# Two-layer hybrid trunk: gate products of three branches as seven block products of summed operands, in place of eight

## The chip, the cores and the metric

One core of one Trainium2 chip. The metric is the device time of one execution in microseconds, as the median of three runs: 1218.11 us before the change (1217.89 to 1218.78). TensorE does the matrix products, ScalarE (ACT), VectorE (DVE) and GpSimd (POOL) the elementwise work, and SyncE (SP) starts most transfers.

## The reference, cut to what matters

```python
for l in range(2):                      # x: 512 latent positions, xc: 256 context positions, 1024 features
    h, hc = modulated_norm(x, xc)       # scale, shift and gate from c and c_ctx (called ada below)
    o_a, o_d, o_b, o_c = attention, windowed attention, Fourier mix, spatial gate   # 256 features each
    y = 0
    for r in (a, d, b, c):              # the merge
        y += sigmoid(h @ w_merge[r] + b_merge[r]) * ((o_r * silu(z_r)) @ w_br[r])
    x = x + gt * (y @ w_out)            # the context has the same, in layer 0 only
```

For each branch, `h @ w_merge[r]` is a product of 1024 features by 1024 outputs over all positions. These gate products are the largest part of the work.

## The kernel before

Features lie on the 128 partitions, positions along the free dimension: columns 0 to 255 are the context, 256 to 767 the latents. Layer 0 works on all 768 columns, layer 1 on the 512 latent ones. Every product is made of three matmuls on rounded parts: weights and activations are split into a high part in fp32r and a low part that is the rest, and `mm3` (L182) issues high x high, high x low and low x high.

Weights come as tiles of 128 x 512 (four blocks of 128 x 128) in the order of a list `plan` (L136). `wload` (L154) starts their transfers on SP's queue, `wround` (L162) splits them: ACT casts the high part (L169), and POOL, or DVE for every third tile, subtracts it (L171). `wnext` (L174) hands out the next tile, five loads and two splits ahead. There are three raw tiles, three high and three low ones.

`merge(r)` (L646) handles one branch in eight steps j, one for each 128 outputs. A step takes two weight tiles of 512 for the gate (8 x 3 matmuls over the latents into bank `gl`, and in layer 0 as many over the context into `gc`) and one of 256 for the branch (2 x 3 matmuls into `yl` and `gc`). Then ACT applies tanh (L669), DVE multiplies by the branch's product, which it reads from PSUM (L671), and the result is added to M: on POOL (L674), or on DVE in the last branch, where the sum is also split into MH and ML for the output product (L680, L681).

The order of the work is written as generators. `drive` (L865) alternates a main thread with a filler: each yield of the main thread adds to a balance, and the filler runs until its own yields, counted as 1.27 per column and triple of matmuls, have used it up. While the two attentions are the main thread (L936), a unit of one head and one query block pays PACE (L27: 4500 and 4000), and the filler is projections, branch C's merge, branch B's input and, last, branch A's merge (L929). What remains of the filler then runs alone (L945). Behind it, branches D and B are merged as the main thread (L951, L954), and the side work is paid 0.42 (SIDE, L31) of what a merge yields. In layer 0 the side is the Fourier mix `fnet` and then `ada_rest` (L248): its rows come as tiles of 128 x 512, and each yield of 1000 stands for one tile and two dot products on DVE (L274), one for each of two vectors. In layer 1 the side is `fnet` alone. The compiler's planner turns this into one order per engine, mostly by when operands are ready in its own estimate; the engines then run in that order.

## Time and profile before

| What | Value |
|---|---|
| Median of three runs | 1218.11 us (1217.89 to 1218.78) |
| The profiled execution, its own time | 1220.09 us |
| Span of the profiled execution, first to last instruction | 1218.2 us |
| TensorE busy | 1183.5 us (97%) |
| DVE busy | 658.7 us (54%) |
| ACT busy | 470.7 us (39%) |
| POOL busy | 392.2 us (32%) |
| Mean granted TensorE clock | 0.994 of full speed |
| Moved by DMA | 131.99 MB, mean 108 GB/s |

All durations below are from the profiled execution. A record's duration includes time that the instruction spends held up after it began. Matmuls overlap in their records, so the time of one is read from the distance of two starts. Times on POOL are rough in the profiler's own words, so they too are best read from start to start.

### The profile page before, as it was taken

What the parts mean: (1) busy time and instruction counts of PE and PEld (TensorE: products, weight loads), DVE (VectorE), ACT (ScalarE), POOL (GpSimd) and SP (SyncE); (2) the same over time, 40 slices, a digit from 0 to 9 for tenths busy, and PEclk for the clock granted to TensorE, in tenths of its full rate; (3) what the DMA queues carried; (4) which work ended last, traced back from release to release, by engine and by line L of the source; (5) the groups of instructions that cost most, each with busy time, mean ns of one, the idle gap of its engine ahead of it and who ended that gap; (6) DMA issues with size and microseconds to landing.
All of it is one profiled execution on the core that took longest, in us unless ns stands there. A gap on an engine that the chain in (4) does not pass through costs nothing.

```text
span 1218.2 us, 18950 instructions
## 1 busy us (share of the span) xinstructions
PE 1183.5 (97%) x7164; PEld 1004.2 (82%) x7164; DVE 658.7 (54%) x1325; ACT 470.7 (39%) x933; POOL 392.2 (32%) x292
## 2 busy tenths in 40 slices
PE   5999999999999999999999998989999999999998
PEld 3798888888888888888888887877788888888887
DVE  5673446443455442588988667646645554232331
ACT  5334634333333332322333255445444444333431
POOL 1322333212212234454222234442222233454332
PEclk8999999999999999999999999999999999999999
DMA  7717213211111113345555653373322212333353
GB/s 282 256 31 172 79 37 83 73 36 61 53 44 49 44 56 83 93 153 160 180 165 193 183 163 110 117 194 75 99 62 69 71 56 77 101 87 100 95 166 124
DMA packets 73499, 131.99 MB, mean 108 GB/s; under 512 B 8769, under 2 KB 19137, under 8 KB 73409
## 3 DMA queue, kind: packets, MB, share of 16 engines
q1 hardware_dynamic: 66640, 120.30, 33.8%
q10 hardware_dynamic: 6768, 10.50, 2.8%
q8 instruction: 56, 0.92, 0.3%
q14 instruction: 35, 0.28, 0.1%
HBM read 115.03 MB, written 4.19 MB: 98 GB/s over the span
## 4 chain that ended last, share of the span: by engine, by line
PE 86%; DVE 5%; DMA 4%; issue 2%; ACT 2%; POOL 1%; SPq 1%; ACTq 0%; POOLq 0%
PE gl L185 10%; PE gl L186 10%; PE gl L188 10%; PE o L631 4%; PE gc L185 3%; PE tp L598 3%; PE gc L188 3%; PE gc L186 3%; PE ow L185 3%; PE ow L186 3%; PE ow L188 3%; PE yl L185 2%; PE yl L186 2%; PE yl L188 2%; PE p L185 2%; PE p L188 2%
## 5 line engine op out<-in xcount | busy, mean ns | idle before, releaser
L171 POOL TENSOR_TENSOR wl<-wr,wh 128x512 fp32r<-128x512 f32 (+1 forms) x222 | 287.5, 1297 | 703.7 <-ACT wh L169 665.4
L169 ACT CAST wh<-wr 128x512 fp32r<-128x512 f32 (+1 forms) x320 | 184.5, 577 | 354.3 <-PE gl L186 92.4
L185 PE MATMUL gl<-hh,wh 128*128 128x512 f32 x512 | 204.2, 399 | 0.0
L186 PE MATMUL gl<-hl,wh 128*128 128x512 f32 x512 | 200.2, 391 | 0.0
L188 PE MATMUL gl<-hh,wl 128*128 128x512 f32 x512 | 199.9, 391 | 0.0
L574 DVE TENSOR_REDUCE mx<-s 128x1 f32<-128x768 f32 (+3 forms) x80 | 61.6, 770 | 131.5 <-PE s L568 67.4
L171 DVE TENSOR_TENSOR wl<-wr,wh 128x512 fp32r<-128x512 f32 (+1 forms) x98 | 68.9, 703 | 116.8 <-ACT wh L169 116.5
L188 PEld LDWEIGHTS gl<-hh,wl 128*128 128x128 f32 x512 | 96.1, 188 | 21.1
L185 PEld LDWEIGHTS gl<-hh,wh 128*128 128x128 f32 x512 | 96.5, 188 | 16.6 <-issue 0.2
L186 PEld LDWEIGHTS gl<-hl,wh 128*128 128x128 f32 x512 | 96.5, 189 | 16.2
L274 DVE CUSTOM_DVE_ANT_0 aj<-at,cb 128x512 f32<-128x512 f32 x128 | 107.1, 876 | 1.5 <-DMA at<-in_wadat_dram 1.5
L582 ACT ACTIVATE p<-s,ng 128x768 f32<-128x768 f32 (+3 forms) x80 | 60.1, 751 | 97.1 <-DVE ng L579 55.5
L185 PE MATMUL gc<-hh,wh 128*128 128x256 f32 x256 | 73.5, 287 | 0.0
L188 PE MATMUL gc<-hh,wl 128*128 128x256 f32 x256 | 72.5, 283 | 0.0
L186 PE MATMUL gc<-hl,wh 128*128 128x256 f32 x256 | 72.3, 283 | 0.0
L185 PE MATMUL p<-hh,wh 128*128 128x512 f32 (+1 forms) x192 | 71.1, 370 | 0.2 <-DVE z L539 0.2
L185 PE MATMUL ow<-MH,wh 128*128 128x512 f32 (+1 forms) x200 | 69.5, 348 | 1.3 <-DVE nq1a L343 0.9
L188 PE MATMUL ow<-MH,wl 128*128 128x512 f32 (+1 forms) x200 | 69.4, 347 | 0.9 <-DVE wl L171 0.9
L186 PE MATMUL ow<-ML,wh 128*128 128x512 f32 (+1 forms) x200 | 69.4, 347 | 0.0
L188 PE MATMUL p<-hh,wl 128*128 128x512 f32 (+1 forms) x192 | 68.4, 356 | 0.0
L186 PE MATMUL p<-hl,wh 128*128 128x512 f32 (+1 forms) x192 | 68.1, 355 | 0.0
L669 ACT ACTIVATE g<-gl,bmh 128x512 f32<-128x512 f32 x64 | 43.8, 685 | 62.2 <-DVE macc L274 37.0
(466 smaller groups left out, 2583.6 us busy)
## 6 DMA issues: line engine op xcount, KB each, us to landing
wr<-in_wm_dram SPq DMA_DIRECT2D x128, 256.0 KB, 2.7
wr<-in_win_dram SPq DMA_DIRECT2D x72, 256.0 KB, 2.9
at<-in_wadat_dram SPq DMA_DIRECT2D x64, 256.0 KB, 2.8
wr<-in_wo_dram SPq DMA_DIRECT2D x40, 256.0 KB, 3.0
aw<-in_wada_dram SPq DMA_DIRECT2D x16, 512.0 KB, 5.8
wr<-in_wm_dram SPq DMA_DIRECT2D x64, 128.0 KB, 2.2
ks<-yk SPq DMA_DIRECT2D x32, 192.0 KB, 4.2
wr<-in_wkv_dram SPq DMA_DIRECT2D x16, 256.0 KB, 2.7
```

Of the source, the lines that this page charges most:

```text
L169: A.copy(hi[:, :n], raw[:, :n])
L171: (V if on_v else G).tensor_sub(lo[:, :n], raw[:, :n], hi[:, :n].bitcast(F32))
L185: T.matmul(d, wh, xh[:, c0:c1], start=first and op, stop=False)
L186: T.matmul(d, wh, xl[:, c0:c1], start=False, stop=False)
L188: T.matmul(d, wl, xh[:, c0:c1], start=False, stop=last and cl)
L274: V.tensor_tensor_reduce(out=junk[:, :512], in0=w[:, :512], in1=cb[2 * v + half][:, :512], scale=0.5, scalar=0.0, op0=ALU.mult, op1=ALU.ad ...
L574: V.reduce_max(out=mx, in_=sv, axis=AX.X)
L582: A.activation(p[:, :nk], sv, AF.Exp, bias=ng, scale=0.125, accum_out=sm_)
L598: T.transpose(tp[:, (i - g0) * P:(i - g0 + 1) * P], p[:, i * P:(i + 1) * P], ident)
L631: T.matmul(dst[64 * hx:64 * hx + 64, :], vt[kt_ // 3][:, kt_ % 3, c0:c0 + 64], pts[hx][:, j * P:(j + 1) * P], start=(j == 0), stop=(j == l ...
L669: A.activation(g[:, q0:q1], gp, AF.Tanh, scale=0.5, bias=bmh[:, r * 8 + j:r * 8 + j + 1])
```

## The change

The gate products of branches A, D and B go from eight block products to seven, by the scheme of Strassen and Winograd. Outputs are taken in pairs (j, j+4), inputs in halves of four slices, and the columns are halved: 384 in layer 0, 256 in layer 1. For each pair, four tiles of weights are summed (two sums on DVE, two on POOL) to give seven tiles of 512 to split in place of four, and seven products of 4 x 3 matmuls over half the columns replace eight. ACT and DVE combine them in three PSUM banks and the gate tiles. The summed activations (`combos`) are made once per layer, with their own high and low parts. Branch C keeps the former merge.

Branch A leaves the attention's filler and is merged behind the attention with D and B, all three with the side work beside them. PACE goes down to 3250 in both layers. There are six raw weight tiles in place of three. `ada_rest` makes only one dot product per tile for the last eight rows of layer 1, whose second value nothing reads. To make room, the rotation's tables are loaded twice per layer into tiles of the z pool, and parts of M, ada's vectors and the next layer's input take tiles of other pools.

The core of the diff (the lists `loads` and `items` replace `plan`: an item is what is split, with its engine in `on_v`):

```diff
-PACE = (4500, 4000)
+PACE = (3250, 3250)
...
-LOADS, W_RAW, W_HI, W_LO = 5, 3, 3, 3
+LOADS, W_RAW, W_HI, W_LO = 5, 6, 3, 3
...
+        def merged_s(l, r):
+            def parts(j):
+                return [(wm[l, r, j, :, :512], 512), (wm[l, r, j, :, 512:1024], 512)]
+            def four(j):
+                (a, b), (c, d) = parts(j), parts(j + 4)
+                return [a, b, c, d]
+            ids = [[load(*x) for x in four(0)]]
+            ys = []
+            for j in range(4):
+                more = four(j + 1) if j < 3 else []
+                y0 = load(wm[l, r, j, :, 1024:], 256)
+                nxt = [load(*x) for x in more[:1]]
+                y1 = load(wm[l, r, j + 4, :, 1024:], 256)
+                nxt += [load(*x) for x in more[1:]]
+                ids.append(nxt)
+                ys.append((y0, y1))
+            for j in range(4):
+                a11, a12, a21, a22 = ids[j]
+                s1 = []
+                def prep(a11=a11, a12=a12, a21=a21, a22=a22, s1=s1):
+                    t = tl("p", f"s1_{a11}")[:, :512]
+                    V.tensor_add(t, raws[a21], raws[a22])
+                    G.tensor_sub(raws[a21], raws[a11], raws[a21])
+                    V.tensor_sub(raws[a11], t, raws[a11])
+                    G.tensor_sub(raws[a12], raws[a12], raws[a11])
+                    s1.append(t)
+                item(a11, 512, on_v=False)
+                item(a12, 512, on_v=True)
+                item(a22, 512, prep, lambda k=a11: raws[k], on_v=False)
+                item(a22, 512, None, lambda k=a21: raws[k], on_v=l == 1)
+                item(a22, 512, None, lambda s1=s1: s1[0], on_v=False)
+                item(ys[j][0], 256, on_v=False)
+                item(a22, 512, None, lambda k=a12: raws[k], on_v=True)
+                item(a22, 512, on_v=False)
+                item(ys[j][1], 256, on_v=False)
...
             for r in (R_A, R_D, R_B):
-                plan += merged(l, r)
-            plan += outw(l)
+                merged_s(l, r)
...
             i = cnt[0]
             cnt[0] += 1
-            wload(i + LOADS)
+            wload(max(k for k, *_ in items[i:i + LOADS]))
             wround(i + 2)
+            while prepped[0] < min(i + 3, len(items)):
+                prep = items[prepped[0]][2]
+                if prep:
+                    prep()
+                prepped[0] += 1
...
-                    for v in range(2):
+                    for v in range(1 if l and j >= 16 else 2):
...
+            HN = (WC.stop - WC.start) // 2
+            H1, H2 = slice(WC.start, WC.start + HN), slice(WC.start + HN, WC.stop)
+            BO = {}
+            def combos():
+                t23 = [[[tl("k", f"T{n}{part}{i}{l}", F32R) for i in range(2)] for part in "hl"] for n in (2, 3)]
+                t4 = [pq.tile([P, 2, NT], F32R, name=f"T4{part}{l}", tag="q") for part in "hl"]
+                def at(ts, kk):
+                    return [t[kk // 2][:, (kk % 2) * HN:(kk % 2) * HN + HN] for t in ts]
+                for n in (11, 21, 22, 1, 2, 3, 4):
+                    BO[n] = []
+                for kk in range(4):
+                    fa, fb = tl("sc", f"fa{l}{kk}"), tl("p", f"fb{l}{kk}")
+                    for f, k_ in ((fa, kk), (fb, kk + 4)):
+                        (V if f is fa else G).tensor_add(f[:, WC], hh[k_][:, WC].bitcast(F32), hl[k_][:, WC].bitcast(F32))
+                    V.tensor_sub(fa[:, H1], fa[:, H2], fa[:, H1])
+                    V.tensor_sub(fa[:, H2], fb[:, H2], fa[:, H2])
+                    V.tensor_sub(fb[:, H2], fb[:, H2], fa[:, H1])
+                    V.tensor_sub(fb[:, H1], fb[:, H1], fb[:, H2])
+                    one = [hh[kk][:, H2], hl[kk][:, H2]]
+                    two, three = at(t23[0], kk), at(t23[1], kk)
+                    four = [t[:, kk // 2, (kk % 2) * HN:(kk % 2) * HN + HN] for t in t4]
+                    for n, (hi, lo), src in ((2, two, fb[:, H2]), (3, three, fa[:, H2]), (1, one, fa[:, H1]),
+                                             (4, four, fb[:, H1])):
+                        A.copy(hi, src)
+                        (G if n < 3 else V).tensor_sub(lo, src, hi.bitcast(F32))
+                        BO[n].append((hi, lo))
+                    BO[11].append((hh[kk][:, H1], hl[kk][:, H1]))
+                    BO[21].append((hh[kk + 4][:, H1], hl[kk + 4][:, H1]))
+                    BO[22].append((hh[kk + 4][:, H2], hl[kk + 4][:, H2]))
+                    yield
...
+            def block(dst, n, start):
+                wh, wl = wnext()
+                for i, (xh, xl) in enumerate(BO[n]):
+                    q = slice(i * P, (i + 1) * P)
+                    T.matmul(dst, wh[:, q], xh, start=start and i == 0, stop=False, skip_group_check=True)
+                    T.matmul(dst, wh[:, q], xl, start=False, stop=False, skip_group_check=True)
+                    T.matmul(dst, wl[:, q], xh, start=False, stop=i == 3, skip_group_check=True)
+                    yield 1.27 * HN
+            def branch(r, j, tags):
+                y_l = bank(f"yl{l}{r}{j}", tags[0])
+                yd = [(y_l, NC, NT, True, True)]
+                if not last:
+                    yd.append((bank(f"yc{l}{r}{j}", tags[1])[:, :NC], 0, NC, True, True))
+                wh, wl = wnext()
+                yield from mmp(yd, wh, wl, YB[r], 0, 2)
+                return yd
+            def merge_s(r, final=False):
+                for j in range(4):
+                    z, x, y = (bank(f"{n}{l}{r}{j}")[:, :HN] for n in "zxy")
+                    g0, g1 = (tl("sc", f"g{l}{r}{i}") for i in (j, j + 4))
+                    bias = [bmh[:, r * 8 + i:r * 8 + i + 1] for i in (j, j + 4)]
+                    def gate(i, jj, g, yd):
+                        for yp, q0, q1, _, _ in reversed(yd):
+                            V.scalar_tensor_tensor(out=g[:, q0:q1], in0=g[:, q0:q1], scalar=1.0, in1=yp,
+                                                   op0=ALU.add, op1=ALU.mult)
+                        (V if final else G).tensor_add(M[jj][:, WC], M[jj][:, WC], g[:, WC])
+                    yield from block(z, 11, True)
+                    A.copy(g0[:, H1], z)
+                    yield from block(x, 21, True)
+                    V.tensor_add(g0[:, H1], x, g0[:, H1])
+                    A.activation(g0[:, H1], g0[:, H1], AF.Tanh, scale=0.5, bias=bias[0])
+                    yield from block(z, 2, False)
+                    A.copy(g1[:, H1], z)
+                    yield from block(y, 3, True)
+                    yield from block(z, 1, False)
+                    A.copy(g1[:, H2], z)
+                    V.tensor_add(g1[:, H2], y, g1[:, H2])
+                    yd = yield from branch(r, j, ("o", "t"))
+                    yield from block(z, 22, False)
+                    A.activation(g0[:, H2], z, AF.Tanh, scale=0.5, bias=bias[0])
+                    gate(0, j, g0, yd)
+                    yield from block(y, 4, False)
+                    V.tensor_add(g1[:, H1], y, g1[:, H1])
+                    A.activation(g1[:, WC], g1[:, WC], AF.Tanh, scale=0.5, bias=bias[1])
+                    yd = yield from branch(r, j + 4, ("t", "o"))
+                    gate(1, j + 4, g1, yd)
...
                 ("mc", lambda: merge(R_C, first=True)), ("z1", lambda: zblock(1)),
-                ("b", bproj), ("ma", ("a0", lambda: merge(R_A))),
+                ("b", bproj),
...
-            drive(paced(merge(R_D, ctag="o"), SIDE), side)
-            while "fnet" not in flags:
-                next(side)
-            drive(paced(merge(R_B, final=True, ctag="o"), SIDE), side)
+            run(combos())
+            for r in (R_A, R_D, R_B):
+                while r == R_B and "fnet" not in flags:
+                    next(side)
+                drive(paced(merge_s(r, final=r == R_B), SIDE), side)
```

## Rows read from the trace of the kernel before

**Rows 1.** The page, busy us (share of the span) of each engine.
```profile
PE 1183.5 (97%) x7164; PEld 1004.2 (82%) x7164; DVE 658.7 (54%) x1325; ACT 470.7 (39%) x933; POOL 392.2 (32%) x292
```

**Rows 2.** Table of waits: TensorE's longest, us in total, times, longest.
```profile
PE n L312 <- DVE sq L310: 7.9, 2, 7.5
```

**Rows 3.** Windows: PE, PEld, DVE, ACT, POOL busy; clock, DMA share, GB/s.
```profile
117.70:456.70 339.00, 337.08 (x2312) 291.23 (x2312) 161.61 (x365) 133.79 (x294) 91.54 (x63) 1.00 0.21 58
456.70:480.80 24.10, 24.10 (x143) 21.37 (x142) 4.35 (x8) 6.78 (x12) 11.89 (x8) 1.00 0.27 73
480.80:572.50 91.70, 91.48 (x546) 81.14 (x546) 65.01 (x145) 27.12 (x51) 41.86 (x27) 1.00 0.45 135
572.50:656.20 83.70, 83.70 (x483) 73.79 (x482) 75.64 (x176) 27.39 (x47) 24.67 (x18) 1.00 0.55 169
1033.20:1057.10 23.90, 23.90 (x108) 19.78 (x107) 5.51 (x8) 8.54 (x15) 11.29 (x11) 1.00 0.35 103
1057.10:1116.40 59.30, 59.30 (x285) 49.93 (x284) 16.82 (x36) 20.43 (x38) 28.64 (x26) 1.00 0.32 91
1116.40:1170.90 54.50, 54.50 (x242) 45.11 (x242) 21.37 (x31) 22.36 (x40) 17.46 (x17) 1.00 0.36 100
```

**Rows 4.** Timeline: same instruction of successive steps; ACT in layer 1, POOL in layer 0.
```profile
1125.99 0.62 ACT L169 CAST wh<-wr 128x512 fp32r<-128x512 f32 x1 [0.28 <-PE gl L186]
...
1132.79 0.62 ACT L169 CAST wh<-wr 128x512 fp32r<-128x512 f32 x1 [0.28 <-PE gl L186]
...
542.56 2.22 POOL L674 TENSOR_TENSOR M<-M,g 128x768 f32<-128x768 f32 x1 [1.42 <-DVE g L671]
...
553.02 2.22 POOL L674 TENSOR_TENSOR M<-M,g 128x768 f32<-128x768 f32 x1 [1.42 <-DVE g L671]
```

**Rows 5.** Timeline of POOL: operations back to back (start, duration).
```profile
1072.29 1.30 POOL L171 TENSOR_TENSOR wl<-wr,wh 128x512 fp32r<-128x512 f32 x1 [3.15 <-ACT wh L169]
1073.55 1.29 POOL L201 TENSOR_TENSOR yb301l<-yf,yb301h 128x512 fp32r<-128x512 f32 x1
...
1077.37 0.73 POOL L171 TENSOR_TENSOR wl<-wr,wh 128x256 fp32r<-128x256 f32 x1
1078.07 1.29 POOL L674 TENSOR_TENSOR M<-M,g 128x512 f32<-128x512 f32 x1
...
506.92 1.93 POOL L201 TENSOR_TENSOR yb300l<-yf,yb300h 128x768 fp32r<-128x768 f32 x1 [1.88 <-ACT yb300h L200]
508.82 1.83 POOL L201 TENSOR_TENSOR yb310l<-yf,yb310h 128x768 fp32r<-128x768 f32 x1
```

**Rows 6.** Timeline of DVE, then POOL, over one stretch of layer 0's branch B.
```profile
574.39 2.32 DVE L274 CUSTOM_DVE_ANT_0 aj<-at,cb 128x512 f32<-128x512 f32 x1
...
577.25 0.41 DVE L171 TENSOR_TENSOR wl<-wr,wh 128x256 fp32r<-128x256 f32 x1
577.59 1.77 DVE L274 CUSTOM_DVE_ANT_0 aj<-at,cb 128x512 f32<-128x512 f32 x1
...
579.29 0.68 DVE L274 CUSTOM_DVE_ANT_0 aj<-at,cb 128x512 f32<-128x512 f32 x1
...
579.90 0.68 DVE L274 CUSTOM_DVE_ANT_0 aj<-at,cb 128x512 f32<-128x512 f32 x1
...
582.52 0.69 DVE L671 SCALAR_TENSOR_TENSOR g<-g,yl 128x512 f32<-128x512 f32 x1
...
573.94 2.22 POOL L674 TENSOR_TENSOR M<-M,g 128x768 f32<-128x768 f32 x1 [1.42 <-DVE g L671]
577.50 1.31 POOL L171 TENSOR_TENSOR wl<-wr,wh 128x512 fp32r<-128x512 f32 x1 [1.34 <-ACT wh L169]
582.65 1.30 POOL L171 TENSOR_TENSOR wl<-wr,wh 128x512 fp32r<-128x512 f32 x1 [3.83 <-ACT wh L169]
```

**Rows 7.** The page, DMA issues: count, KB each, us to landing.
```profile
wr<-in_wm_dram SPq DMA_DIRECT2D x128, 256.0 KB, 2.7
```

More of the change, by code (lines that the diff above doesn't have):

```diff
@@ L119, in hybrid_trunk, with load, item, pieces @@
         x2d = pd.tile([P, KT, NL], F32, name="x2d")
+        TAB = []
         STQ = nc.sync
         cnt = [0]
+        loads, raws, items = [], {}, []
+        def load(src, n):
+            loads.append((src, n))
+            return len(loads) - 1
+        def item(k, n, prep=None, get=None, on_v=None):
+            items.append((k + 1, n, prep, get or (lambda: raws[k][:, :n]), on_v))
+        def pieces(ps):
+            for src, n in ps:
+                item(load(src, n), n)
         def blocks(l, *bs):
-            return [(win[l, b, :, h * 512:h * 512 + 512], 512) for b in bs for h in range(2)]
+            pieces([(win[l, b, :, h * 512:h * 512 + 512], 512) for b in bs for h in range(2)])
@@ L146, in hybrid_trunk @@
             for r in (R_A, R_D, R_B):
-                plan += merged(l, r)
-            plan += outw(l)
+                merged_s(l, r)
+            outw(l)
             if l == 0:
-                both[0] = len(plan)
-                plan += outw(l, WHOLE)
-        loaded, ready = [], []
+                both[0] = len(items)
+                outw(l, WHOLE)
+        ready, prepped = [], [0]
         def wload(upto):
-            while len(loaded) < min(upto, len(plan)):
-                i = len(loaded)
-                src, n = plan[i]
-                raw = pw.tile([P, 512], F32, name=f"wr{i}", tag="wraw", bufs=W_RAW)
-                nc.sync.dma_start(raw[:, :n], src)
-                loaded.append(raw)
+            for k in range(len(raws), min(upto, len(loads))):
+                src, n = loads[k]
+                raws[k] = pw.tile([P, 512], F32, name=f"wr{k}", tag="wraw", bufs=W_RAW)
+                nc.sync.dma_start(raws[k][:, :n], src)
@@ L162, in wround @@
         def wround(upto):
-            while len(ready) < min(upto, len(plan)):
+            while len(ready) < min(upto, len(items)):
                 i = len(ready)
-                n, raw = plan[i][1], loaded[i]
+                _, n, _, get, on_v = items[i]
+                raw = get()
                 hi = pw.tile([P, 512], F32R, name=f"wh{i}", tag="whi", bufs=W_HI)
                 lo = pw.tile([P, 512], F32R, name=f"wl{i}", tag="wlo", bufs=W_LO)
-                A.copy(hi[:, :n], raw[:, :n])
-                on_v = i % 3 == 0 if both[0] <= i < both[1] else i % 3 == 2 and i >= 24
-                (V if on_v else G).tensor_sub(lo[:, :n], raw[:, :n], hi[:, :n].bitcast(F32))
+                A.copy(hi[:, :n], raw)
+                if on_v is None:
+                    on_v = i % 3 == 0 if both[0] <= i < both[1] else i % 3 == 2 and i >= 24
+                (V if on_v else G).tensor_sub(lo[:, :n], raw, hi[:, :n].bitcast(F32))
@@ L271, in ada_rest @@
                     nc.sync.dma_start(w[:, :512], wadat[l, j, :, half * 512:half * 512 + 512])
-                    for v in range(2):
+                    for v in range(1 if l and j >= 16 else 2):
                         junk = tl("sc", f"aj{l}_{j}_{half}{v}")
                         V.tensor_tensor_reduce(
-                            out=junk[:, :512], in0=w[:, :512], in1=cb[2 * v + half][:, :512], scale=0.5,
+                            out=junk[:, :512], in0=w[:, :512], in1=cb[2 * v + half], scale=0.5,
                             scalar=0.0, op0=ALU.mult, op1=ALU.add, accum_out=macc[l][:, j, v, half:half + 1])
@@ L453, in vproj, with tables @@
                     sink(t, accs[j // 2][:, (j % 2) * 256:(j % 2) * 256 + 256])
+            def tables(name):
+                if not TAB:
+                    for i in range(2):
+                        t = tl("z", f"rt{i}{name}")
+                        nc.scalar.dma_start(t[:, :NL], krope[:, i * NL:(i + 1) * NL])
+                        TAB.append(t[:, :NL])
+                return TAB
             class Rope:
@@ L644, in hybrid_trunk, with merge @@
             MH, ML = [None] * KT, [None] * KT
-            def merge(r, first=False, final=False, ctag="mm"):
+            def merge(r, first=False):
                 yb = YB[r]
-                mlp = mq = None
                 for j in range(KT):
```

74 lines of the change are left out of this document (37 added, 37 removed).

## The prediction

> **What bounds the kernel now.** I read the page's busy shares first: TensorE is busy in 1183.5 of 1218.2 us [rows 1]. The table of waits confirms it: TensorE's longest wait is 7.9 us in all, at the start [rows 2]. Then the windows by stage: both attentions and all merges that the change touches have TensorE busy end to end [rows 3]. So before the change a matmul that goes away is time that goes away, and every other engine has slack. The question is whether that slack covers what the change adds to DVE and POOL. That is not read from their busy times, but from what one does to the other.
>
> **The products.** Period of one merge step in layer 1: 6.80 us for 30 matmuls of 512 columns, 0.2267 us each. In layer 0 a step takes 10.46 us, with 30 more of 256 columns: (10.46 - 6.80)/30 = 0.122 us each [rows 4]. The 384-column blocks of layer 0 have no row of their own kind; between the two, half way, 0.174 us.
> A pair (j, j+4) has 48 gate matmuls of each width now and 84 narrower ones after. Layer 0: 48 x 0.3487 = 16.74 us against 84 x 0.174 = 14.64. Layer 1: 48 x 0.2267 = 10.88 against 84 x 0.122 = 10.25. The branch products stay: 4.18 and 2.72 us. For TensorE alone a pair goes from 20.92 to 18.82 us and from 13.60 to 12.97; 12 pairs in each layer give -25.2 and -7.6, together -33 us. At 256 columns the overhead of a matmul eats half of the eighth.
> The Trainium skill (TensorE: Matmul & The Clock Gate, Back-to-back issue gap) gives 131 ns for 512 columns and 81 for 128 in a sustained stream. On a straight line between them, my estimate, 84 narrow blocks in layer 1 would cost more than 48 wide ones: 8.2 against 6.3 us. The trace disagrees (0.2267 and 0.122 us), and the sum above goes by the trace.
>
> **What is paid for it, pair by pair.** Weight tiles to split go from 4 to 7 per pair, with four sums of weights ahead of them. POOL then has, per pair: five 512-wide low parts in layer 0 (four in layer 1, where the fourth tile goes to DVE), two 256-wide ones, two weight sums, and two additions into M in branches A and D. Back to back POOL takes 1.25 us for 512, 0.70 for 256 and about 1.80 for 768 elements (1.90 from the first 768 row to the next start, 1.83 the length of the second) [rows 5]. Layer 0, A and D: 5 x 1.25 + 1.4 + 2.5 + 3.6 = 13.8 us; layer 1: 4 x 1.25 + 1.4 + 2.5 + 2.5 = 11.4. In B the additions are DVE's: 10.2 and 8.9.
> Each alone would fit under 18.8 and 13.0. But DVE and POOL do not run side by side. The ada dot product (two SBUF inputs) is 0.68 us long and follows itself after 0.61. Where a POOL operation is on the way it takes 2.32 or 1.77 us, and each time it ends about 0.55 us after POOL's record: POOL 573.94 + 2.22 = 576.16, DVE 574.39 + 2.32 = 576.71; POOL 577.50 + 1.31 = 578.81, DVE 577.59 + 1.77 = 579.36 [rows 6]. POOL's 2.22 is itself a wait, as its like takes 1.80. DVE's gate step, whose second input is PSUM, keeps its 0.69 beside a POOL operation [rows 6]. So DVE operations with both inputs in SBUF and POOL operations must be added up on one resource, which I call the port.
> The Trainium skill says the same (SBUF — State Buffer, Who interferes with whom): an exclusive lock for the whole instruction; an addition of PSUM and SBUF would stay free of it.
> Port per pair, DVE at 0.61 us for 512 and 0.34 for 256 [rows 6], 0.88 for 768 on the same slope. Two low parts and two sums of weights are 2.44 us. Layer 0, A and D: 13.8 + 2.4 = 16.2. B, where M's two additions and its two rounding steps are DVE's: 10.2 + 2.4 + 4 x 0.88 = 16.1. Layer 1 has one low part more: A and D 11.4 + 3.05 = 14.45; B 8.9 + 3.05 + 4 x 0.61 = 14.4.
>
> **Layer 1.** The port needs 14.4 us where TensorE needs 13.0 and the pair takes 13.6 now. Floor for three branches: 12 x 14.4 + 4.8 (the Fourier products, as D's window is longer than B's by 4.8 [rows 3]) = 178, against 12 x 13.60 + 4.8 = 168: +10 us. Beyond the floor there is a burst. From the end of the seventh product to the low part of the next pair's third one, TensorE has 6.0 us of work; in it POOL must do two M additions, two low parts and two weight sums (7.5 us) and DVE two sums and a low part (1.8), after 0.8 us for a cast (0.62 [rows 4] and its release): 10.1, a stall of 4.1 in A and D; in B, with four and five operations, 8.9 and 2.9. In full that is 8 x (13.0 + 4.1 - 13.6) + 4 x (13.0 + 2.9 - 13.6) = +37. But it is partly filled, since only the third matmul of a column block needs the low part; and what queues in the burst is served in the quiet rest of the pair. I take +14, near the floor, bounds +10 and +37. The raw tile that the sums wait for last can be asked for once the seventh tile is split, 2.7 us before it lands [rows 7], and is there before the port is free. The loads themselves stay as many: 1.28 MB per pair in 14 to 19 us, and ada's, on SP's queue that carries 169 GB/s in B today [rows 3].
>
> **Layer 0.** The side work adds ada dot products to the same port. Each merge pays 0.42 x 1.27 per column into the side: 7.37 thousand per pair after. The Fourier part and ada's start cost 13 thousand (1.8 pairs); then 48 steps of two dot products (6.5 pairs) and 16 of one (2.2 pairs), since the change drops the unused half of the last 16. A step costs one thousand, so 7.37 steps or 9.0 us of port per pair: 16.2 + 9.0 = 25.2 us against TensorE's 18.8. Sum: 1.8 x 18.8 + 8.0 (Fourier, D's 91.7 less B's 83.7 [rows 3]) + 6.5 x 25.2 + 2.2 x 20.6 + 1.5 x 18.8 = 279. If backlog evens out perfectly, the port's total holds: 8 x 16.2 + 4 x 16.1 + 112 x 0.61 + 6 = 268. Now: 3 x 83.7 + 8.0 = 259. I take +13, bounds +9 and +20. DVE is in order: a dot product that waits for POOL holds the low parts queued behind it, and TensorE waits for those.
>
> **Sums of activations.** Before branch A, for each of 4 slices: an addition and a low pair on POOL, an addition, four differences and two low parts on DVE. Port in layer 0, with 0.98 and 0.48 for 384 elements half way between the rows' sizes: 4 x (1.80 + 2 x 0.98 + 0.88 + 6 x 0.48) = 30 us; layer 1: 4 x (1.25 + 1.4 + 0.61 + 6 x 0.34) = 21. The third product needs all second sums, about 0.85 of it. Cover: the first two products (4.2 and 2.9 us), the Fourier products (8.0 and 4.8), and filler left after the attention. That filler is 24.1 and 23.9 us now [rows 3]. A's merge leaves it (83.7 and 54.4), and the lower pace takes 48 x 1250 and 32 x 750 less of it, at 1.046 us per 975 units 64 and 26 us: 5 us and none remain. Stall 25 - 17 = 8 and 18 - 8 = 10; some of it can start before the attention ends, so 6 and 9; bounds 0 to 20 and 3 to 18.
>
> **The attention.** A unit of layer 0 shrinks from 339/48 = 7.06 us to 5.7. DVE and ACT are busy 161.6/48 = 3.4 and 2.8 us of it [rows 3], so neither binds: +2 us, bounds 0 and 8.
> **At nothing:** tables of the rotation loaded twice, ada's rows in other tiles, other tags for M's parts and xn: these lie beside dense TensorE work. Six raw tiles in place of three are what the sums of weights need.
>
> **Sum.** 14 + 13 + 15 + 2 = +44 us; the 33 us of TensorE are inside the stage sums. The profiled execution took 1220.1 us (span 1218.2), 2 above the median 1218.1: 1262 by the median. All lower bounds give 1218 + 10 + 9 + 3 = 1240; upper bounds in all of them at once, 1218 + 37 + 20 + 38 + 8 = 1321, are unlikely together, and I close the case at 1300.
>
> **Rivals.** *TensorE stays the bound* (the other side). If DVE and POOL can share, POOL's 13.8 and 11.4 us fit under 18.8 and 13.0, and only a start-up of about 10 us is paid: 1218 - 33 + 10 = 1195. It decides where port per pair is under 18.8 and 13.0. For it: before the change the layer 0 B stage carries DVE 75.6 and POOL 24.7 of 83.7 us without a stall of TensorE [rows 3]. Against it: part of those 75.6 is waiting, as rows 6 show; without waiting a step there needs 2 x 1.25 on POOL and 0.34 + 2 x 0.88 + 8.2 x 0.61 on DVE, 9.6 us of port per 10.46.
> *Only POOL's queue binds, in layer 1:* the burst there without the lock is six operations and 0.8 us, 8.3 against 6.0, 2.3 us per pair, of which the gain takes 0.6; layer 0 gains its 25. 1218 - 25 + 6 + 12 x 1.7 + 9 = 1228.
> *Attention loses its cover:* if a unit cannot go below today's length, 64 + 26 us come on top: about 1350.
>
> **How the numbers follow.** Forecast 0.62 (1240 to 1300), POOL alone 0.12, TensorE 0.22, attention 0.04. Range 1202 to 1300: it takes in the first two and the slower end of the third. About 0.2% is what a measurement can tell from no change: faster 0.22, same 0.04, slower 0.74.
>
> **What would show it.** Right: in the layer 1 merges TensorE waits for low parts and POOL and DVE together are busy beyond the window's length; pairs of 14.5 us or more; in layer 0 pairs of 22 to 25 us while dot products run and 19 after; long dot-product records beside POOL. Wrong: TensorE dense in the merges at 18.8 and 13.0 us per pair; or idle inside the attention.

## The result: 13% slower, and the profile after

The changed kernel takes 1374.71 us (median of four runs, 1368.8 to 1376.6) where the kernel before took 1218.44 beside it: 1.127 times as long, 95% interval 1.124 to 1.131. The forecast was slower, 1262 us, with a range of 1202 to 1300. The sign was right; of the loss of 156 us it held 44.

The page of the changed kernel, its header, TensorE's part of the first table, and its busy tenths and granted clock (tenths of full speed) in 40 slices, against [rows 1]:

```profile
span 1373.3 us, 20249 instructions
PE 1203.5 (88%) x7452; PEld 1041.8 (76%) x7452; DVE 822.3 (60%) x1481; ACT 548.3 (40%) x1109; POOL 564.9 (41%) x424
...
PE   6899999999991987778889999989999858788889
...
PEclk9999999999995999999999999999999969999899
```

TensorE has 288 matmuls more than before, the gate's narrower ones; its busy time rose by 20 us where the forecast had it fall by 33. It now idles 170 us (1373.3 less 1203.5) where it had idled 35. Two slices stand out, the 13th and the 33rd: the ends of the two attentions.

The windows by stage (columns as in [rows 3]) are layer 0's attention, the gap behind it, layer 0's three merges; then all up to the end of layer 1's attention (not shown), its gap and its merges:

```profile
122.80:417.40 294.60, 289.65 (x2011) 246.83 (x2009) 158.21 (x354) 118.30 (x267) 68.90 (x49) 0.99 0.19 54
417.40:445.40 28.00, 2.47 (x10) 2.21 (x11) 27.57 (x30) 9.98 (x20) 19.28 (x14) 0.50 0.03 9
445.40:747.40 302.00, 251.59 (x1328) 228.97 (x1328) 224.96 (x410) 103.67 (x193) 178.49 (x125) 0.95 0.38 116
...
1093.40:1115.20 21.80, 2.07 (x9) 1.78 (x8) 20.28 (x32) 7.84 (x21) 14.83 (x14) 0.59 0.09 24
1115.20:1326.10 210.90, 174.47 (x1166) 161.11 (x1166) 100.48 (x149) 93.74 (x190) 136.52 (x113) 0.94 0.27 77
```

To set these against [rows 3], A's merge has to be added to the branches behind the attention (8 steps by 10.46 and 6.80 us, [rows 4]) and taken from what is ahead of it. The account of the 155 us by which the span grew:

| stretch | after | before, A moved | more | forecast |
|---|---|---|---|---|
| up to layer 0's attention (varies from run to run) | 122.8 | 117.7 | 5.1 | 0 |
| layer 0's attention and gap | 322.6 | 279.4 | 43.2 | 8 |
| layer 0's merges | 302.0 | 259.1 | 42.9 | 13 |
| output, layer 1's attention and gap | 367.8 | 346.5 | 21.3 | 9 |
| layer 1's merges | 210.9 | 168.2 | 42.7 | 14 |
| last output | 47.2 | 47.3 | -0.1 | 0 |

TensorE's longest waits (us in total, times, longest), against [rows 2]:

```profile
PE gcs L945 <- DMA kd<-in_kdft_dram: 44.6, 2, 24.9
PE z L786 <- POOL wl L229: 38.4, 31, 5.8
PE z L784 <- ACT g L816: 12.4, 8, 2.2
PE x L786 <- DVE wl L229: 10.9, 13, 1.8
```

The first line is the two gaps, in which DVE is busy nearly from end to end (27.57 of 28.00 us and 20.28 of 21.80). The rest are the waits within the pairs, most of them for low parts from POOL.

One pair of each kind, between the starts of x's first product in successive pairs: layer 0 with 14 dot products and with one; then in layer 1 the first pair of branch D, a steady one, and one of branch B:

```profile
516.80:543.60 26.80, 20.45 (x109) 17.91 (x108) 23.50 (x43) 7.89 (x15) 16.90 (x11) 1.00 0.40 123
702.20:724.50 22.30, 19.47 (x110) 18.13 (x109) 14.88 (x22) 10.05 (x18) 10.88 (x8) 1.00 0.18 54
1184.10:1204.70 20.60, 15.04 (x98) 13.91 (x97) 8.74 (x11) 7.45 (x15) 14.73 (x12) 0.92 0.24 65
1220.90:1237.00 16.10, 13.57 (x98) 12.45 (x97) 7.35 (x11) 7.46 (x15) 11.94 (x10) 1.00 0.26 74
1287.80:1306.90 19.10, 15.86 (x98) 14.95 (x97) 10.10 (x15) 8.46 (x17) 8.65 (x7) 0.82 0.22 63
```

The forecast had 25.2, about 19, then 14.4 for the rest. Where dot products are few, or none, a pair is 2 to 6 us above it.

### The profile page after: what moved, and what is told of

Read it like the earlier page. It is cut to its first block, busy times and chain, and to the rows that moved or that the text cites. A ratio compares the mean times of both kernels' runs of the same rounds, so it can differ in the third digit from the quotient of the medians.

```text
span 1373.3 us, 20249 instructions
## 1 busy us (share of the span) xinstructions
PE 1203.5 (88%) x7452; PEld 1041.8 (76%) x7452; DVE 822.3 (60%) x1481; ACT 548.3 (40%) x1109; POOL 564.9 (41%) x424
## 5 line engine op out<-in xcount | busy, mean ns | idle before, releaser
L229 POOL TENSOR_TENSOR wl<-wr,wh 128x512 fp32r<-128x512 f32 (+1 forms) x258 | 327.6, 1274 | 590.5 <-ACT wh L226 564.1
L229 DVE TENSOR_TENSOR wl<-wr,wh 128x512 fp32r<-128x512 f32 (+1 forms) x110 | 88.7, 806 | 107.6 <-ACT wh L226 106.8
L784 PE MATMUL z<-hh,wh 128*128 128x384 f32 (+1 forms) x288 | 92.0, 320 | 12.4 <-ACT g L816 12.4
L786 PE MATMUL z<-hh,wl 128*128 128x384 f32 (+1 forms) x288 | 92.3, 320 | 5.0 <-POOL wl L229 4.7
L785 PE MATMUL z<-hl,wh 128*128 128x384 f32 (+1 forms) x288 | 91.0, 316 | 0.0
L784 PEld LDWEIGHTS z<-hh,wh 128*128 128x128 f32 x288 | 56.2, 195 | 16.1 <-ACT g L816 14.9
L786 PEld LDWEIGHTS z<-hh,wl 128*128 128x128 f32 x288 | 55.9, 194 | 7.9 <-POOL wl L229 7.3
L785 PEld LDWEIGHTS z<-hl,wh 128*128 128x128 f32 x288 | 56.2, 195 | 1.2 <-issue 0.3
L665 PE MATMUL tp<-kconst,p 128*128 128x128 f32 x368 | 54.0, 275 | 2.5 <-DVE ng L646 1.3
L698 PE MATMUL o<-pt,vt 128*64 128x128 f32 x736 | 54.3, 281 | 1.4 <-DVE pt L667 1.3
L808 POOL TENSOR_TENSOR M<-M,g 128x768 f32<-128x768 f32 (+1 forms) x32 | 53.5, 1671 | 3.5 <-DVE g L806 3.5
```

The costliest lines, as they stand in the source:

```text
L229: (V if on_v else G).tensor_sub(lo[:, :n], raw, hi[:, :n].bitcast(F32))
L698: T.matmul(dst[64 * hx:64 * hx + 64, :], vt[kt_ // 3][:, kt_ % 3, c0:c0 + 64], pts[hx][:, j * P:(j + 1) * P], start=(j == 0), stop=(j == l ...
L784: T.matmul(dst, wh[:, q], xh, start=start and i == 0, stop=False, skip_group_check=True)
L785: T.matmul(dst, wh[:, q], xl, start=False, stop=False, skip_group_check=True)
L786: T.matmul(dst, wl[:, q], xh, start=False, stop=i == 3, skip_group_check=True)
```

## The experiments

The theories. **P**: DVE's operations on two SBUF inputs and POOL's exclude one another, and their sum sets the pair (the forecast's own). **Q**: sums made in place wait until the other engine has read the old value. **R**: the loss sits in the two gaps. **C**: the half clock behind a stall. Each kernel is the changed one with the edit shown (cut to its main lines), one time each. The changed kernel's own four times lie 8 us apart, and the attention of layer 0 begins anywhere from 116.1 to 122.8 us in these traces, whatever the edit; so a difference of less than about 6 us counts only where the trace shows where it lies.

**No sums of weights.**
```diff
-                item(a22, 512, prep, lambda k=a11: raws[k], on_v=False)
+                item(a22, 512, None, lambda k=a11: raws[k], on_v=False)
...
-                item(a22, 512, None, lambda s1=s1: s1[0], on_v=False)
+                item(a22, 512, None, lambda k=a22: raws[k], on_v=False)
```


> Leaves out the four weight sums of each pair: the products read the weights as loaded. Theory P: a pair gives back two sums on POOL by 1.25 us and two on VectorE by 0.70, 3.9 us, down to TensorE's own time: layer 1 from 16.1 to 13.0 to 13.5, layer 0 from 25 to 27 to 21.5 to 23; 12 pairs by 3 and 12 by 3.5, about 1295 to 1305. Theory Q gives the same or a little more, down to the floor. Theory R: the steady pairs matter little, 1350 to 1370.

Measured 1278.49 us, 96 less: more than P had asked for. Windows of one pair of layer 0 with dot products, one without, and one of layer 1:

```profile
481.40:503.90 22.50, 19.68 (x110) 18.17 (x110) 20.52 (x38) 8.00 (x15) 12.95 (x10) 1.00 0.48 135
664.70:683.50 18.80, 18.80 (x110) 18.27 (x109) 10.80 (x18) 9.59 (x17) 9.01 (x8) 1.00 0.24 64
1096.40:1109.20 12.80, 12.80 (x98) 12.29 (x97) 6.49 (x9) 7.41 (x15) 9.48 (x9) 1.00 0.35 94
```

TensorE has no gap left at 18.80 and 12.8 us, so the forecast's price of the products (18.82 and 12.97) holds, and the four sums of each pair are the largest single cause.

**Merges on VectorE alone.**
```diff
-                    G.tensor_sub(raws[a21], raws[a11], raws[a21])
+                    V.tensor_sub(raws[a21], raws[a11], raws[a21])
...
-                item(a11, 512, on_v=False)
+                item(a11, 512, on_v=True)
...
-                        (V if final else G).tensor_add(M[jj][:, WC], M[jj][:, WC], g[:, WC])
+                        V.tensor_add(M[jj][:, WC], M[jj][:, WC], g[:, WC])
...
```
The other sums and low parts of the merges move in the same way.

> All of the computation is kept; inside the merges the weight sums, the low parts and the additions to M all run on VectorE and none on POOL. Theory P: without POOL nothing lengthens VectorE's records, which then sum to 14.3 us a pair of layer 0 (17.2 with four dot products) and about 11 us of layer 1, under TensorE's 18.8 and 13.0: pairs of 18.8 to 20 and of 13 to 13.5 us, 1265 to 1285 us. Rival S (one queue is worse than two: low parts stand behind gate operations that wait for products): pairs of 20 to 25 and 15 to 17 us, 1330 to 1400. Theory R alone: 1350 to 1375.

Measured 1315.01 us, 60 less, with every operation kept: between P's range and S's. DVE's groups over 110 us of layer 1's merges, 1130 to 1240 in either run (busy us, mean ns | idle before them): first the changed kernel's low parts and in-place difference,

```profile
L229 DVE TENSOR_TENSOR wl<-wr,wh 128x512 fp32r<-128x512 f32 x20 | 19.4, 970 | 30.8 <-ACT wh L226 30.5
L176 DVE TENSOR_TENSOR wr<-s,wr 128x512 f32<-128x512 f32 x7 | 11.2, 1607 | 8.7 <-POOL wl L229 8.7
```

then the same shapes without POOL, and one steady pair of layer 1:

```profile
L229 DVE TENSOR_TENSOR wl<-wr,wh 128x512 fp32r<-128x512 f32 x44 | 31.0, 709 | 12.1 <-ACT wh L226 12.1
L176 DVE TENSOR_TENSOR wr<-s,wr 128x512 f32<-128x512 f32 x8 | 5.5, 681 | 0.0
```
```profile
1173.80:1187.70 13.90, 13.69 (x99) 12.56 (x98) 11.22 (x21) 7.49 (x15) 0.00 (x0) 1.00 0.32 86
```

One engine does 21 operations in 11.2 us where two had needed 7.35 and 11.94 for the same work and still kept TensorE waiting. L176 falls from 1607 to 681 ns, the low parts from 970 to 709. The shorter records are P. But the edit also puts all sums and low parts into one queue, so no sum waits for the other engine any more (the idle time before L176 falls from 8.7 us to nothing), which is Q; this run doesn't part the two. Rival S (the single queue) falls in layer 1. Layer 0 came only to 21 to 26 us, and there the expectation was wrong: it had counted four dot products to a pair, the trace has 14 to 16 in most, and by 0.70 us these take the estimate from 17.2 to about 25 us of DVE. That is too much in turn: in a pair of 23.0 us with 16 of them DVE is busy for 21.5.

**The same, with the dot products spread further.**
```diff
-SIDE = 0.42
+SIDE = 0.28
```


> All of the computation is kept; merges without POOL as in the run at 1315.0 us, and the work beside them handed out at two thirds of the rate, so that some 10 dot products stand in a pair of layer 0 in place of 14 to 16 and the rest in the output stage behind it (167 us, VectorE busy 100). Theory P: layer 0's pairs of 23 to 25 us hold 25 us of VectorE, and lose 5 dot products by 0.70: 21 to 22 us, 12 to 20 us in all, 1295 to 1303. Rival: the dot products run into the norm's operations at the end of the layer and are paid there, 1310 to 1330.

Measured 1321.02 us: the rival. Layer 0's pairs did come down, seven of them to within 0.5 us of TensorE's floor; but the stretch from the merges' end to layer 1's first pair grew from 342.9 to 373.7. One pair of layer 0, and TensorE's wait in the norm behind the output:

```profile
569.00:587.80 18.80, 18.80 (x110) 18.27 (x109) 18.18 (x42) 8.24 (x15) 0.00 (x0) 1.00 0.44 134
```
```profile
PE n1a L401 <- DVE nq1a L380: 13.1, 1, 13.1
```

So the pair does reach its floor when DVE's work fits under it; but the dot products have no cheap place behind it.

**VectorE alone, the rate between, the Fourier branch held back.**
```diff
-SIDE = 0.42
+SIDE = 0.36
...
+                m = paced(merge_s(r, final=r == R_B), SIDE)
+                if r == R_A:
+                    for _ in range(8):
+                        next(m)
```


> All of the computation is kept; merges on VectorE alone (1315.0 us), the Fourier branch held back for two blocks, and the work beside at 0.36 between the 0.42 of the change and the 0.28 that moved 30 us into the output stage. Theory P: layer 0's pairs near 20 to 21, the output stage 343 to 350 us to the next merges, 1290 to 1300. If every dot product moved is paid in full later: 1310 to 1320.

Measured 1309.42 us, just under the second case and outside the first. It is the best version that computes all, with layer 0's pairs at 18.8 to 26 us. It is 91 us slower than the kernel before, and the gaps alone (28.1 and 20.3 us idle in the two first pairs) are half of that.

**Short dot products.**
```diff
-                            out=junk[:, :512], in0=w[:, :512], in1=cb[2 * v + half], scale=0.5,
+                            out=junk[:, :8], in0=w[:, :8], in1=cb[2 * v + half][:, :8], scale=0.5,
```


> Leaves out most of layer 0's dot products behind the attention: each runs over 8 of its 512 columns. Theory P (VectorE's operations on two SBUF inputs and POOL's exclude one another, so their sum sets the pair): the pairs of layer 0 that carry dot products (25 to 27 us) fall to the 22.3 to 22.9 us of those that carry none, 8 pairs by 3.5 us, about 1345 us. Theory Q (the sums made in place: each waits until the other engine has read the old value): the dot products are not in that chain, at most 10 us, 1365 to 1375. Theory R (the loss sits in the two gaps and in the half clock after a stall): 1360 to 1375.

Measured 1351.88 us, 23 less: near P's number, far beyond Q's and R's. The pairs that carry dot products fell from 25 to 27 us (one 30) to 22 to 26 (one 27), and stopped there: without the dot products' length they still stand 3 to 8 us above the floor of 18.8.

**No sums of activations.**
```diff
-                    V.tensor_sub(fa[:, H1], fa[:, H2], fa[:, H1])
...
+                for n, o, h in ((11, 0, H1), (21, 4, H1), (22, 4, H2), (1, 0, H2), (2, 4, H2), (3, 0, H1), (4, 4, H1)):
+                    BO[n] = [(hh[kk + o][:, h], hl[kk + o][:, h]) for kk in range(4)]
```


> Leaves out the sums of the activations: the seven products read existing halves of the normed input. Theory R: both gaps (28.0 and 21.8 us with TensorE idle) go, and with them the half clock behind them, 50 to 60 us, 1315 to 1325. The forecast's terms (6 us in layer 0, 9 in layer 1): about 1360. Theory P adds nothing of its own here: the later pairs keep 25 to 27 and 16.1 us.

Measured 1332.72 us, 42 less, the time of the two gaps less what then waits for weights. The forecast had priced it at 15. The first pair shrinks from 66.5 to 39.4 us in layer 0 and from 44.1 to 26.5 in layer 1; the later pairs keep their 25 to 27 (one 30) and 16.1.

**Weight sums in tiles of their own** (on top of the run before).
```diff
-                    G.tensor_sub(raws[a21], raws[a11], raws[a21])
-                    V.tensor_sub(raws[a11], t, raws[a11])
-                    G.tensor_sub(raws[a12], raws[a12], raws[a11])
+                    d1, d2, d3 = (tl("k", f"d{i}_{a11}")[:, :512] for i in range(3))
+                    G.tensor_sub(d1, raws[a11], raws[a21])
+                    V.tensor_sub(d2, t, raws[a11])
+                    G.tensor_sub(d3, raws[a12], d2)
...
```


> To be read against the run without sums of activations (1332.7 us), which it also leaves out; here the four weight sums of a pair are written to tiles of their own in place of over the weights, with the same instructions on the same engines. Theory Q: the sums no longer wait for the low parts of the old values on the other engine: layer 1's steady pairs fall from 16.1 to the 14.4 to 14.9 of the forecast's sum over both engines, layer 0's by 1 to 2, together 27 to 39 us, 1295 to 1308. Theory P alone: the same instructions exclude one another as before, 1325 to 1335.

Measured 1310.71 us, 22 less with the same operations on the same engines: between the two numbers, nearer Q's. What Q means is seen in the changed kernel's timeline of a steady pair of layer 1 (start, duration, line, and in brackets the idle time before and who ended it), DVE, POOL, and TensorE's wait at the end:

```profile
1216.23 0.69 DVE L174 TENSOR_TENSOR s<-wr,wr 128x512 f32<-128x512 f32 x1 [1.69 <-DMA wr<-in_wm_dram]
...
1219.56 1.76 DVE L176 TENSOR_TENSOR wr<-s,wr 128x512 f32<-128x512 f32 x1 [1.54 <-POOL wl L229]
1221.25 0.68 DVE L229 TENSOR_TENSOR wl<-wr,wh 128x512 fp32r<-128x512 f32 x1
```
```profile
1218.26 1.27 POOL L229 TENSOR_TENSOR wl<-wr,wh 128x512 fp32r<-128x512 f32 x1
1219.49 1.29 POOL L808 TENSOR_TENSOR M<-M,g 128x512 f32<-128x512 f32 x1
1222.00 1.29 POOL L177 TENSOR_TENSOR wr<-wr,wr 128x512 f32<-128x512 f32 x1 [1.23 <-DVE wl L229]
1223.26 1.71 POOL L229 TENSOR_TENSOR wl<-wr,wh 128x512 fp32r<-128x512 f32 x1
```
```profile
1225.02 0.39 PE L786 MATMUL z<-T2h,wl 128*128 128x256 f32 x1 [1.34 <-POOL wl L229]
```

DVE's L176 overwrites the first weight block and so waits 1.54 us until POOL's low part (L229) has read it; it starts just behind POOL's addition to M and runs into it, 1.76 us in place of 0.68. POOL's L177 then overwrites the second block and waits 1.23 us for DVE's low part of that. TensorE waits at the end of that chain. At its head stands a load: DVE is idle for 1.69 us until the last of the four raw blocks lands (L174), and in the run with own tiles it waits 2.3 to 3.5 us for it in most pairs of layer 1. The forecast had it there before the port is free. In the pair shown POOL still makes low parts for most of that time, so the load holds up the chain by some 0.3 us; no run here varies it. With own tiles the steady pairs take 15.4 to 15.9 us, still above the forecast's 14.45. Of the 22 us layer 1 has 19, and 9 of these lie in three of its pairs, the first two and the first of branch D, which also ran at a higher clock (0.90 to 1.00 in place of 0.77 to 0.87); in the steady pairs own tiles are worth 0.3 to 1.2 us each.

**The Fourier branch held back for two blocks.**
```diff
-                drive(paced(merge_s(r, final=r == R_B), SIDE), side)
+                m = paced(merge_s(r, final=r == R_B), SIDE)
+                if r == R_A:
+                    for _ in range(8):
+                        next(m)
+                drive(m, side)
```


> All of the computation is kept; the work beside the merges (the Fourier branch first) is held back until the first pair's first two blocks are issued, which need no sum of activations. Reading 1: the sums themselves end the gap, and TensorE only gets 24 products into it: 4 us in layer 0 and 3 in layer 1, 1362 to 1372. Reading 2: the Fourier tables' load, on which the trace puts both gaps (44.6 us), is itself the late one because it stood first in TensorE's queue: the gaps fall by half or more, 1345 or less.

Measured 1366.54 us: reading 1's number, though not by its way. The gaps stayed (44.3 us on the same wait, the longest 24.8). The two blocks that need no sum had been run already, among the attention's last units, in both kernels. Of the 8 us, 4.3 are a start that came earlier (118.5 against 122.8 us to the attention), which the edit doesn't touch. Reading 2 falls.

**The tables asked for first.**
```diff
+            for _ in range(4):
+                next(side)
             run(combos())
```


> All of the computation is kept; the Fourier branch's tables are asked for, and its first twelve products issued, ahead of the sums of activations in place of behind them. Reading F (the forecast's cover of 8.0 and 4.8 us was lost because the tables came late): the wait on the tables (44.6 us) goes, TensorE has work in the gaps, about 13 us less, 1355 to 1363. Reading V (the gaps last as long as VectorE has sums to make, whatever TensorE could do): the same idle time is put on another wait, on the sums' tiles, and the time stays within 5 us, 1365 to 1380.

Measured 1365.27 us, 9 less, at the edge of V's interval and short of F's. The waits it has in place of the one on the tables:

```profile
PE mid L971 <- DVE mid L976: 19.5, 1, 19.5
PE df L984 <- DMA tab<-in_dfl_dram: 11.1, 1, 11.1
```
```profile
419.90:444.30 24.40, 4.93 (x23) 4.55 (x21) 24.32 (x30) 9.30 (x19) 14.78 (x12) 0.50 0.01 3
```

TensorE is busy for 4.93 us in layer 0's gap in place of 2.47 and then waits 19.5 us for a two-column operation of DVE that stands behind the sums in DVE's queue. DVE is busy in 24.32 of 24.40 us. So layer 0's gap is DVE's, as V has it; the name of the wait said who came last, not who was slow. The 11.1 us are layer 1's: the load of a second table, which ACT's queue started only at 1105.94 us, between casts for the sums and just after it had waited for one of DVE's low parts (T4l, L773). Some 5 and 4 us of cover were to be had in the first pairs (idle 24.3 and 17.0 us in place of 29.4 and 20.7); the attention begins as late as in the changed kernel (122.2), so these are the 9 us.

**All three left out.** The three edits above together.

> Leaves out all three: sums of activations, weight sums, and most of layer 0's dot products; what remains of the change is the seven products, their snapshots and gates, and the merge of A moved behind the attention. If these three hold the loss: 1218 less the 33 us of products saved, and with the 16 us that the start and layer 0's attention had lost: 1200 to 1212. If the order of the pair (a snapshot or gate that TensorE waits for) costs by itself, 1225 to 1250.

Measured 1207.22 us: within the first case. The three together are worth 167.5 us, singly 22.8 + 42.0 + 96.2 = 161. The page, and layer 1's merges from the second pair on:

```profile
span 1205.4 us, 19951 instructions
PE 1161.0 (96%) x7452; PEld 1021.3 (85%) x7452; DVE 678.4 (56%) x1377; ACT 537.0 (45%) x1077; POOL 449.8 (37%) x352
```
```profile
1011.70:1158.30 146.60, 142.46 (x1047) 135.80 (x1046) 75.21 (x102) 84.69 (x173) 98.44 (x83) 0.99 0.36 102
```

With all sums free of charge, and most of layer 0's dot products too, which the kernel before does make, the change gains 13 us on the 1220.10 us of the kernel before measured beside it. That is about the most it could give in this form; the best kernel that makes the sums takes 102 us more. The first pair of branch D in layer 1 is still slow here, without any sum of weights:

```profile
1051.50:1069.00 17.50, 14.37 (x98) 13.65 (x97) 6.48 (x9) 7.62 (x16) 12.07 (x11) 0.90 0.27 76
1069.00:1081.90 12.90, 12.90 (x99) 12.38 (x98) 6.58 (x9) 7.41 (x15) 9.58 (x9) 1.00 0.37 102
```

**A's merge back among the attention's products** (on top of the run before; pace as before the change).
```diff
-                ("b", bproj),
+                ("b", bproj), ("ma", ("a0", lambda: merge(R_A))),
...
-            for r in (R_A, R_D, R_B):
+            for r in (R_D, R_B):
```


> As the run at 1207.2 us without the three kinds of sums, but A's merge is made in the old way among the attention's products, and the attention is paced as before; D and B keep the seven products. Theory M (A's products were the attention's cover, and moving them costs 11 us in layer 0's attention and 5 at its start and end): 1207 and the 11 us of products that A no longer saves, less 16: about 1202. If the move cost nothing: about 1218.

Measured 1236.79 us, neither of the two. From the attention's start to the end of layer 0's merges it takes 527.6 us, the run at 1207.2 takes 528.4, though that one saves a third of layer 0's 25.2 us on A: in that stretch the move of A cost some 9 us of cover. But with eight pairs in place of twelve to hide in, the side work ran on into the output stage, where TensorE is busy in 157.60 of 184.80 us (in the run at 1207.2 in 173.88 of 183.00); that is worth more than what was asked, so as a whole the run settles nothing.

**Spare products at the stalls.**
```diff
+                    if spare is not None and i == 0:
+                        for _ in range((10, 6)[l]):
+                            T.matmul(spare, hh[0][:, H1.start:H1.start + P], hh[0][:, H1.start:H1.start + 512 - HN],
+                                     start=True, stop=True, skip_group_check=True)
                     T.matmul(dst, wl[:, q], xh, start=False, stop=i == 3, skip_group_check=True)
```


> All of the computation is kept; three blocks of each pair get extra products whose result nobody reads (10 of 128 columns in layer 0, 6 of 256 in layer 1, into the spare columns of y's bank) ahead of the first product that needs the weight's low part, where TensorE waits. Theory C (stalls bring the granted clock down to half for the products behind them): the stalls shorten, the pairs that ran at a clock of 0.82 to 0.92 come near those at 1.00 (17.8 to 20.7 us to 16.1 to 17 in layer 1), 15 to 25 us in all, 1350 to 1360, although some 2.2 us of products are added to each pair of layer 1. Without theory C the products either hide in TensorE's waits (1370 to 1380) or add up to 20 to 45 us, 1395 to 1420.

Measured 1413.07 us, 38 more: they add up. The steady pair goes from 16.1 to 17.1 us, and pairs at a low clock stay (19.6 us at 0.91). This remedy fails, which says nothing against theory C itself; what the half clock costs is left to the rows below.

## Why the forecast was wrong, step by step

**Held.** The products: 18.80 and 12.84 us per pair in the runs where TensorE is dense, against 18.82 and 12.97. The port: DVE's records shrink from 970 and 1607 ns to 709 and 681 when POOL is away, and a pair of layer 0 with dot products takes 25 to 27 us (one 30), against the forecast's 25.2. Laid over one another, POOL's records and those of DVE with two SBUF inputs cover 24.7 us of the layer 0 pair shown above (26.8 us) and 14.5 of the steady pair of layer 1 (16.1 us): the forecast's sums of 25.2 and 14.45 hold. The Trainium skill (SBUF — State Buffer, Who interferes with whom) states the lock; these records agree. The rival *TensorE stays the bound* fails by that, and *only POOL's queue binds* too: without the lock DVE's records would not shrink.

**The step that failed most: cover for the sums of activations** (15 us in the forecast, 42 by the run without them). The forecast's work was right: 30 us of port in layer 0 and 21 in layer 1, where the records of the sums, DVE's and POOL's laid over one another, cover 32.2 and 20.5, and the gaps last 28.0 and 21.8. The cover was wrong. It had set 17 us against layer 0's (two products, the Fourier products, 5 of filler) and 8 against layer 1's. The filler and the two products were used up by the attention's last units. The Fourier products came late: the loads of their tables stood in ACT's queue among the casts for the sums (in layer 0 that of `kd` was started at 440.1 us), and with the tables asked for first they still waited for small operations of DVE, which stood in line behind the sums. Of the 8.0 and 4.8 us that the forecast had set for them, that run got some 5 and 4. The forecast treated TensorE's work as cover without asking which engine must feed it.

**The pairs** (27 us in the forecast for both layers, 86 in the account). Three parts were missed. First, the order: the forecast took a pair as long as the port's work, as if the order were free, with the burst "near the floor". But 16.1 us stands where the sum gives 14.45: the port is idle for 1.7 us of a steady pair and later keeps TensorE waiting. Sums in place are a part of this, as own tiles give back some; what else there is of it stays open. Second, work that the forecast left out: in branch D's first pair (20.6 against 16.1 us, TensorE waiting 3.8 in one piece), POOL must also make the low parts of the Fourier branch's product (L264), which comes out of the side work just then. They stand ahead of the low parts (L229) that TensorE needs:

```profile
1183.93 1.73 POOL L264 TENSOR_TENSOR yb301l<-yf,yb301h 128x512 fp32r<-128x512 f32 x1
1186.29 1.29 POOL L177 TENSOR_TENSOR wr<-wr,wr 128x512 f32<-128x512 f32 x1 [0.63 <-DVE wl L229]
1187.54 1.71 POOL L264 TENSOR_TENSOR yb311l<-yf,yb311h 128x512 fp32r<-128x512 f32 x1
1189.22 1.26 POOL L808 TENSOR_TENSOR M<-M,g 128x512 f32<-128x512 f32 x1
1190.43 1.26 POOL L229 TENSOR_TENSOR wl<-wr,wh 128x512 fp32r<-128x512 f32 x1
```

The sums of weights are not its cause: the run at 1207.2 us has none, and there the same pair takes 17.5 us against 12.8, with the same two operations ahead. The first pair of branch B, where nothing of the kind is due, takes 16.7. Third, the granted clock. The matmuls of the run at 1207.2 us and of the changed kernel are the same 7452; they are busy for 1161.0 and 1203.5 us. Weighting TensorE's busy stretches with the clock granted in them, over the whole trace, gives an estimate of what half speed cost: 36.3 us in the changed kernel, 11.7 in that run and 5.8 before, so 25 of the 42.5. The rest fits the tails of products where the stream breaks off: at a clock of 1.00, the steady pair has TensorE busy in 13.57 us with its stalls and in 12.80 without.

**The attention and the start** (2 us in the forecast). The attention's stretch is 15 us longer than before without A, 4 of it products of A run ahead. The other 11 (upper bound given: 8) I put down to its last units, which stand bare once the filler is out: TensorE is idle for 4.0 us after 400 us and for 1.0 in all of the stretch before that. No run tries this by itself. The 5 us ahead of the attention are no step of the forecast's: that start lies between 116.1 and 122.8 us in the changed kernel and the runs made from it, with the same code ahead of it. Eleven of these thirteen starts are later than the 117.7 of the one trace from before, so the change may cost some 2 us here, for a reason that no run shows.

**The bounds.** All upper bounds at once gave 1321 and I closed the range at 1300, as unlikely together. They were not independent: most are work of DVE and POOL on one port with TensorE waiting, and the clock comes down behind some of the waits. The rival with the attention's loss named a time of about 1350 for another reason; the attention gave 11 us, not 90.

## What to carry to other kernels

Trading an eighth of TensorE's products for sums on other engines pays only where those sums are hidden; here a gain of 33 us on paper had a ceiling of 13, and the sums cost 167 with the dot products beside them. When work is to hide behind TensorE's, follow each of those products back to the engine that feeds it: if it is the engine that is busy, there is little cover. List all that an engine has in its queue at that time, the side work's operations too, and not only what the change adds. Before splitting work over DVE and POOL, try it on DVE alone; two engines on one port can be slower than one.

## What the runs showed of the hardware

**The granted clock after waits.** In the steady pair, with waits of 0.70 and 1.34 us, the clock stays at 1.00. In the first pair of branch D, waits of 1.78 and 3.78 us (1.7 us of products between) are followed by full clock up to 1193.1 and then by 0.50, the lower of the two levels, with products of 256 columns 0.21 us apart in place of 0.12; then it is full again. In branch B, with two shorter waits (1.31 and 1.93 us, half a microsecond of products between), the clock fell at 1292.1, during the second, and stayed at 0.50 for longer. The windows: the waits (in D the longer one) and the stretches at half clock, D first, then B:

```profile
1187.00:1193.00 6.00, 2.22 (x19) 2.02 (x18) 1.46 (x2) 1.13 (x2) 5.93 (x5) 1.00 0.03 8
1193.15:1196.45 3.30, 3.30 (x18) 3.30 (x17) 0.11 (x1) 1.29 (x3) 0.73 (x1) 0.50 0.62 169
...
1289.30:1292.00 2.70, 0.63 (x4) 0.30 (x2) 2.70 (x5) 2.54 (x5) 1.84 (x2) 1.00 0.00 0
1292.10:1298.90 6.80, 5.74 (x27) 5.74 (x28) 1.71 (x2) 1.31 (x4) 3.43 (x3) 0.50 0.33 95
```

In D, TensorE is dense in the 3.30 us at half clock: that price is paid after the wait, in products that wait for nothing, so the table of waits does not show it. The Trainium skill (TensorE: Matmul & The Clock Gate, HAM oscillation — how this bites in real kernels) describes a loop whose wait brings the clock down in each turn; here it came down in some pairs and not in others of the same code.

**One engine beside two.** For the 21 operations of a pair of layer 1, DVE alone needs 11.22 us; with POOL helping, the two are busy for 7.35 and 11.94, and the pair takes 2.2 us longer, the waits between the two queues included.
